# A hybrid decoder layer: more places for two weight streams, pinned scale steps two units apart, transpositions a unit later

## The chip, the cores and the metric

The kernel runs on one core of one Trainium2 chip. The metric is device time in microseconds (us). A core has five engines with a queue each, worked in order: TensorE (PE, with its weight loads as PEld), VectorE (DVE), ScalarE (ACT), GpSimd (POOL) and SyncE (SP), whose queue here issues most DMAs. Matmuls write to PSUM, a memory of eight banks per partition; the other operands lie in SBUF.

## What is computed

One layer, 2048 positions of width 1024, in float32 from outside. Cut to what matters:

```
mod = silu(c) @ w_ada + b_ada          -> sh1, sc1, g1, sh2, sc2, g2
h   = rmsnorm(x) * (1 + sc1) + sh1
q, k, v, forget, x_in, B, C = split(h @ w_in)
q, k = rmsnorm per head (8 heads of 64)
attn = causal attention with logits q.k/8 + F[t] - F[s],  F = cumsum(log sigmoid(forget + b))
conv = B * causal_dwconv3(C * x_in)
x   = x + g1 * (concat(attn, conv) @ w_out)
h2  = rmsnorm(x) * (1 + sc2) + sh2
u   = causal_dwconv3(h2 @ w_up);  x + g2 * ((silu(u_gate) * u_val) @ w_down)
```

## The kernel before, in words

A float32 product is made of three products of parts: each operand is split into a high and a low half, and high x high, high x low and low x high are added in one PSUM bank (`mm3`, L140). In the input projection most parts are float16. So that they fit float16's range, each group of weight columns is first scaled by a power of two that is worked out on the chip, and so is h.

**The planner.** The kernel is written with a framework that orders the instructions of each engine itself, by a model of their times: an instruction that is ready early can be put ahead of others that stand before it in the program. `K` (L138) pins an instruction behind the one traced before it on its engine. All of TensorE's instructions around the change are pinned, most of VectorE's and ScalarE's are not. A pool gives each tag a number of places (`bufs`); a tile waits until the last reader of its place is done.

**Value stage** (some 20 to 163 us). A loop over k = 0 to 9 makes, for each 128 rows of w_ada's first two parts, the modulation of that slice (`modulation`, L288; its columns a1 and sh1), transposes chunk 0 of x (512 positions) to h (`transpose_in`, L345), and adds the products for the values of the first three tiles of 128 positions (`value_products`). In the last rounds `normalize` (L329) squares the tiles of the next chunk on ScalarE and works out their reciprocal roots on VectorE in small steps (`rsqrt_steps`). `rest()` is the low half of h's chunk 0 (L356). Chunk 0 is multiplied in split float32, the other chunks in float16. For these `first_scales` (L368) works out two scales, of h and of the value columns: sums and maxima on VectorE (L372 to L376), a transposition (L170), a maximum (L172, L173), a small product that spreads it (L176), five small steps to the power of two (L177 to L181), then a1 and sh1 times the scale (L382, L383) and eight splits of value weights (L195 on ScalarE, L196 on VectorE). It is a generator: each `next` does a part of it. Before, its first part stood after the loop and the rest in tile 3 at k = 2. Then come 16 tiles of 128 positions; the chunks 1 to 3 are normalized and transposed between their products (L348 on TensorE, L350 on ScalarE, L136 on POOL and L353 on VectorE for the halves).

**Keys and queries** (163 to 361 us). `project` (L601) runs over 16 units, tiles of 128 positions: 24 matmuls (L142), then the squares on ScalarE (L632), sums and reciprocal roots on VectorE (L634 to L637) and the normalized tile qn (L638). `finish` (L603) transposes a qn on TensorE (L606), scales it (L612 on ScalarE), makes halves (POOL, and L614 on VectorE) and stores them by SP's queue (L616). It is called at the end of a unit's products for the tile of two units before. The dictionary of hooks puts small steps at the end of given units: the sums of the forget gates (`running_sum`, `running_offset` with the product L525), the scales of gains and values (`largest_value` with the transposition L562, and others). In the query stage each unit also loads a tile of values, splits and stores it (L578, L583, L584).

**Groups of weights.** `weight_group` (L198) is a generator that loads a group, sums magnitudes, then goes through the chain L170 to L181 in two parts, one `next` apart, and then makes the splits, one per `next`. The group of the queries is prepared during the keys, that of a conv group during the stage before it.

**Conv groups** (361 to 626 us). Four groups of 128 channels, four chunks each, and per chunk the products x, c and b (24 matmuls each); after each product one `next` of the following group. Then the gating and the convolution on POOL and VectorE (L796 to L816), and a store by ScalarE's queue.

**Two streams beside these stages.** `magnitudes` (L704) loads w_up in 88 tiles `wx` of 128 x 512 and adds up their absolute values on ScalarE (L708), for a scale of later use; it is called twice in most units and after most products of a conv group. `piece` (L691) goes through 16 pieces of the rest of w_ada: `modulate` (L654) loads eight tiles `wm` of 128 x 256, adds them up on VectorE (L662, L664), and returns a step that finishes the sum on TensorE (L669 or L684) at the next call. Calls stand in the query stage after units 3, 6, 9, 12 and 15 and in each conv chunk but the first. `wx` has one place and `wm` two.

**PSUM.** The tag "tr" has two places (`ps_t`); every transposition and every small product named here takes one until VectorE or ScalarE has read it. Accumulators have six.

At (j, ch) = (3, 2) the pool of the attention's queries and keys is opened on the right side of SBUF, and head 0's are loaded (L757) and copied by POOL (L766). The stages after 626 us (attention, output projection, ConvFFN) are not touched.

Of the kernel before, what the change touches and what calls it, by code (L numbers as in the profile page):

```python
# [45 lines left out]
def kernel(  # L46
# [102 lines left out]
    with ExitStack() as ph:  # L149
# [16 lines left out]
        def power_of_two(pool, m, s, top):  # L166
# [5 lines left out]
            V.tensor_reduce(top[:, 0:1], pt[0:n, 0:P], axis=AX.X, op=ALU.max)  # L172
            V.tensor_scalar(top, ident[0:n, 0:n], top[:, 0:1], None, op0=ALU.mult)  # L173
# [3 lines left out]
            V.tensor_scalar(s, pt[:, 0:n], 2.0**-18, 2.0**40, op0=ALU.max, op1=ALU.min)  # L177
            V.tensor_scalar(s.bitcast(I32), s.bitcast(I32), 0x7F800000, None, op0=ALU.bitwise_and)
            V.reciprocal(s, s)
            V.tensor_scalar(s.bitcast(I32), s.bitcast(I32), 0x7F800000, None, op0=ALU.bitwise_and)  # L180
            V.tensor_scalar(s, s, 4096.0, None, op0=ALU.mult)  # L181
# [16 lines left out]
        def weight_group(srcs, shape, tag):  # L198
# [7 lines left out]
            def steps():  # L206
# [11 lines left out]
                yield  # L218
                next(chain, None)
# [3 lines left out]
                for raw in raws:  # L223
# [4 lines left out]
                    yield  # L228
# [8 lines left out]
        def conv_group(j):  # L237
# [5 lines left out]
                [P, 4, P], ("wh", "wl")[j % 2],  # L243
            )

        with ExitStack() as pa:
# [121 lines left out]
            def first_scales():  # L368

                t, u = [ap.tile([P, KD], F32, tag=n, name="abs") for n in ("abs_a", "abs_s")]  # L370
                for src, dst in ((a1, t), (sh1, u)):
                    V.tensor_scalar(dst, src, -1.0, None, op0=ALU.mult)  # L372
                    V.tensor_tensor(dst, dst, src, op=ALU.max)
                V.scalar_tensor_tensor(t, t, 32.0, u, op0=ALU.mult, op1=ALU.add)
                V.tensor_reduce(hm[:, 0:1], t, axis=AX.X, op=ALU.max)
                V.tensor_reduce(hm[:, 1:2], wsum, axis=AX.X, op=ALU.max)  # L376
# [4 lines left out]
                V.tensor_copy(rh, hs[:, 0:1])  # L381
                V.tensor_scalar(a1, a1, rh, None, op0=ALU.mult)  # L382
                V.tensor_scalar(sh1, sh1, rh, None, op0=ALU.mult)  # L383
                for k in range(KD):
# [3 lines left out]
                    wv16.append(pair)  # L388
                unscale(hs[:, 1:2], hm[:, 0:1], hm[:, 1:2])
# [6 lines left out]
            early = [[ps_m.tile([P, 512], F32, tag="mm", name="pv") for _ in range(2)] for _ in range(3)]  # L396
            for k in range(KD + 2):
                if k < KD:
                    modulation(k, () if k else normalize(0))
                if 0 < k <= KD:  # L400
                    rest()
                if k < KD:
                    rest = transpose_in(0, k)
                if k == KD - 1:
                    load_x(1)
                    load_x(2)
                    norms = normalize(1)
                    next(norms)
# [1104 lines left out]
```

## Time and profile before

| | |
|---|---|
| median of 3 runs | 2441.19 us (2439.45 to 2441.63) |
| profiled execution, its own time | 2440.35 us |
| its span, first to last instruction | 2438.5 us |
| mean granted TensorE clock | 0.995 |
| loads of wx: count, KB each, issue to landing | 88, 256.0, 2.8 us |
| loads of wm: count, KB each, issue to landing | 128, 128.0, 2.7 us |
| one sum of wx on ScalarE (L708) | 629 ns |

The profile shows one execution. A row of waits reads: engine, line and tile of the instruction that waited, what ended the wait, total us, number of waits, longest. A row of a timeline reads: start and length in us, engine, line, operation, output and inputs, sizes, count, and in brackets the idle time before it and what ended it. Busy times of TensorE come from modelled ends of pipelined matmuls. A granted clock below 1.00 means that TensorE ran slower in that stretch.

### The profile page before, as it was taken

Reading aid. Unit: us, or ns where it says so; the run is one execution under the profiler, and the core shown is the slowest. Engines: PE = TensorE matmul, PEld = TensorE weight load, DVE = VectorE, ACT = ScalarE, POOL = GpSimd, SP = SyncE. Lnnn points to the kernel's source line nnn. Section 1 sums busy time; section 2 is a strip of 40 time slices with the busy share of each in tenths; the row PEclk is TensorE's granted clock in tenths of the full one; section 3 lists DMA queues with packets and bytes.
Section 4 is the critical chain, followed back from the end, with each engine's and each line's share of the span. In section 5 each row is a group of like instructions: output and inputs, shape, how many; then the busy total and the mean of one; then the engine's idle time right before and its main releaser. Section 6 shows DMA issues by size and latency. Waiting matters only on the chain.

```text
span 2438.5 us, 38643 instructions
## 1 busy us (share of the span) xinstructions
PE 2336.2 (96%) x14472; PEld 1405.9 (58%) x14472; DVE 1802.1 (74%) x3430; ACT 1307.1 (54%) x2136; POOL 338.6 (14%) x282
## 2 busy tenths in 40 slices
PE   5899989999899998999999999999999999999999
PEld 5764444444577776444444444788864444448887
DVE  6767785553799898456888888757768888985554
ACT  5644454321588897343665665554546556554333
POOL 0210101111577784001000000000000000000000
PEclk9999999999999999999999999999999999999999
DMA  9337687541599997534222222676742222236775
GB/s 278 126 105 193 156 244 208 157 127 44 109 182 187 227 183 144 179 108 151 82 92 87 87 87 86 201 247 217 229 134 87 87 87 88 92 103 210 229 227 183
DMA packets 428707, 368.71 MB, mean 151 GB/s; under 512 B 184208, under 2 KB 327912, under 8 KB 427496
## 3 DMA queue, kind: packets, MB, share of 16 engines
q1 hardware_dynamic: 421400, 349.40, 51.4%
q10 hardware_dynamic: 4752, 8.46, 1.0%
q0 software_dynamic: 2368, 8.39, 0.9%
q8 instruction: 113, 1.85, 0.3%
q14 instruction: 74, 0.61, 0.1%
HBM read 267.54 MB, written 65.08 MB: 136 GB/s over the span
## 4 chain that ended last, share of the span: by engine, by line
PE 72%; DVE 4%; ACT 2%; issue 2%; DMA 1%; POOL 0%; SPq 0%; ACTq 0%; DVEq 0%
PE acc L1360 33%; PE acc L142 24%; PE pr L142 6%; PE pt L1041 2%; PE ps L980 1%; PE ps L981 1%; DVE near L1048 1%; PE po L1077 1%; PE po L1079 1%; PE po L1078 1%; ACT s_t L1021 1%; DMA far<-wide 1%; DVE s_t L1004 1%; PE pt L1201 1%; DVE t L1177 0%
## 5 line engine op out<-in xcount | busy, mean ns | idle before, releaser
L1360 PEld LDWEIGHTS <-pair 128*128 128x128 f16 x3696 | 361.4, 98 | 436.3 <-issue 0.3
L1360 PE MATMUL acc<-t,pair 128*128 128x512 f16 x2112 | 477.4, 379 | 0.0
L1360 PE MATMUL acc<-b,pair 128*128 128x512 f16 x1584 | 363.5, 379 | 0.0
L1332 DVE TENSOR_TENSOR lo<-raw,hi 128x1024 fp32r<-128x1024 f32 x176 | 212.0, 1224 | 154.2 <-ACT hi L1331 153.9
L142 PE MATMUL acc<-hi 128*128 128x512 f32 x704 | 277.0, 394 | 1.6 <-DVE t L1177 1.5
L1331 ACT ACTIVATE hi<-raw 128x1024 fp32r<-128x1024 f32 x176 | 182.3, 1055 | 177.5 <-PE acc L142 142.4
L142 PE MATMUL acc<-lo,hi 128*128 128x512 f32 x704 | 274.5, 390 | 0.5 <-DVE lo L1332 0.5
L142 PE MATMUL acc<-hi,lo 128*128 128x512 f32 x704 | 274.4, 390 | 0.0
L1373 DVE SCALAR_TENSOR_TENSOR w<-w,fcw,w 128x1024 f32<-128x1024 f32 x176 | 226.1, 1285 | 34.6 <-ACT w L1368 25.2
L142 PEld LDWEIGHTS <-h 128*128 128x128 f16 x1344 | 130.6, 98 | 98.8 <-DVE h L353 4.6
L1184 ACT ACTIVATE pair<-raw 128x1024 f16<-128x1024 f32 x132 | 138.3, 1049 | 68.4 <-DVE raw L1267 68.4
L1368 ACT ACTIVATE w<-w,fcw 128x1024 f32<-128x1024 f32 x88 | 100.7, 1144 | 130.7 <-DVE w L1266 130.7
L142 PE MATMUL acc<-wp,mp 128*128 128x512 f16 x768 | 169.4, 379 | 1.1 <-DVE raw L933 1.0
L1021 ACT ACTIVATE s_t<-s_t,nb,cst 128x2048 f32<-128x2048 f32 (+15 forms) x128 | 164.7, 1288 | 5.1 <-ACT nb L1018 0.4
L1187 DVE TENSOR_TENSOR pair<-raw,pair 128x1024 f16<-128x1024 f32 x132 | 160.9, 1219 | 4.7 <-ACT pair L1184 4.7
L708 ACT ACTIVATE wx<-wx 128x512 f32<-128x512 f32 x88 | 55.4, 629 | 178.8 <-DMA wx<-in_w_up_dram 156.1
L142 PEld LDWEIGHTS acc<-hi 128*128 128x128 f32 x704 | 132.2, 188 | 31.4 <-DVE t L1177 4.4
L142 PEld LDWEIGHTS acc<-hi,lo 128*128 128x128 f32 x704 | 132.2, 188 | 27.8
L142 PEld LDWEIGHTS acc<-lo,hi 128*128 128x128 f32 x704 | 132.3, 188 | 27.5 <-DVE lo L1332 1.1
L1033 POOL TENSOR_TENSOR wide<-s_t,wide 128x1024 f16<-128x1024 f32 x64 | 136.7, 2136 | 5.3
L1004 DVE CUSTOM_DVE_ANT_0 s_t<-ps,nf,mx 128x512 f32<-128x512 f32 (+1 forms) x192 | 119.5, 644 | 16.6 <-PE ps L983 8.2
L142 PE MATMUL pr<-h,wl 128*128 128x512 f16 x576 | 127.0, 382 | 0.0
(344 smaller groups left out, 4212.3 us busy)
## 6 DMA issues: line engine op xcount, KB each, us to landing
raw<-in_w_up_dram SPq DMA_DIRECT2D x88, 512.0 KB, 3.7
raw<-y_sc SPq DMA_DIRECT2D x176, 256.0 KB, 4.1
raw<-in_w_down_dram SPq DMA_DIRECT2D x176, 256.0 KB, 5.9
wx<-in_w_up_dram SPq DMA_DIRECT2D x88, 256.0 KB, 2.8
y_sc<-w SPq DMA_DIRECT2D x44, 512.0 KB, 2.6
wm<-in_w_ada_dram SPq DMA_DIRECT2D x128, 128.0 KB, 2.7
wr<-in_w_in_dram SPq DMA_DIRECT2D x40, 256.0 KB, 4.2
x_t<-in_x_dram SPq DMA_DIRECT2D x16, 512.0 KB, 4.6
```

The lines of the kernel that those rows point to most:

```text
L142: ins = T.matmul(acc, lhsT=a, rhs=b, start=st, stop=sp)
L708: K(A.activation(t, t, AF.Abs, accum_out=l1[:, n : n + 1]))
L1004: K(V.tensor_tensor_reduce(out=s_t[:, o0 + c0 : o0 + c0 + cw], in0=ps[:, 0:cw], in1=nf[:, c0 : c0 + cw], scale=1.0, scalar=-3.0e38 if g == ...
L1021: K(A.activation(cols, cols, AF.Exp, bias=nb[:, p : p + 1], scale=qk[:, 4:5], accum_out=un["l"][:, p : p + 1]))
L1033: K(G.tensor_tensor(wide[:, 1, :], s_t[:, WB * P : WU], wide[:, 0, :], op=ALU.subtract))
L1184: K(A.activation(hi, raw, AF.Copy))
L1187: K(V.tensor_tensor(lo, raw, hi, op=ALU.subtract))
L1331: K(A.activation(hi, raw, AF.Copy))
L1332: K(V.tensor_tensor(lo, raw, hi.bitcast(F32), op=ALU.subtract))
L1360: K(T.matmul(acc, lhsT=a, rhs=b, start=st, stop=sp, skip_group_check=True))
L1368: K(A.activation(y, u[:, 0:1024], AF.Copy, scale=fcw[:, ct : ct + 1]))
L1373: K(V.scalar_tensor_tensor(y, u[:, m : m + 1024], fcw[:, m * 44 + ct : m * 44 + ct + 1], y, op0=ALU.mult, op1=ALU.add))
```

## The change

Five things are changed together.

- `wm` gets 16 places and `wx` four, in a pool of their own on the right side, which is closed where the attention's pool is opened. A piece's eight tiles are loaded at one call, summed at the next, and finished at the one after that; a tile of w_up is summed when three are loaded.
- In `weight_group` one more `next` lies between the two parts of the scale chain, and the conv groups from the second on make two splits per `next`.
- The VectorE instructions of the scale chains are pinned with `K`.
- `first_scales` starts in the value loop (parts at k = 7, 8 and 8), and its last four splits follow in tile 3 at k = 0; `normalize(1)` starts at k = 8, behind the last `rest()`.
- `finish` is called when three tiles of qn wait rather than two; qn has four places; three tiles are left over at the end of each projection. `running_offset` moves from unit 5 to unit 4.

The diff, without the lines that only gain a `K(...)` (L172, L173, L177 to L181, L372 to L376, L381 to L383):

```diff
-        def weight_group(srcs, shape, tag):
+        def weight_group(srcs, shape, tag, at_once=1):
...
                 next(chain)
                 yield
+                yield
                 next(chain, None)
...
-                for raw in raws:
+                for n, raw in enumerate(raws, 1):
...
-                    yield
+                    if n % at_once == 0:
+                        yield
...
-                [P, 4, P], ("wh", "wl")[j % 2],
+                [P, 4, P], ("wh", "wl")[j % 2], 2 if j else 1,
...
+                yield
                 chain = power_of_two(ps_t, hm, hs, htop)
                 next(chain)
                 yield
                 next(chain, None)
...
+                yield
                 for k in range(KD):
...
                     wv16.append(pair)
+                    if k == 3:
+                        yield
...
+            first = first_scales()
             for k in range(KD + 2):
                 if k < KD:
                     modulation(k, () if k else normalize(0))
                 if 0 < k <= KD:
+                    if k == KD:
+                        next(first)
                     rest()
...
                     load_x(2)
+                    next(first)
+                if k == KD:
                     norms = normalize(1)
                     next(norms)
                 if k >= 2:
                     for t in range(3):
                         value_products(early[t], 0, t, k - 2)
+                        if k == KD and t == 1:
+                            next(first)
...
-            first = first_scales()
             next(first)
             pin(norms)
...
-                            if (i, k) == (3, 2):
+                            if (i, k) == (3, 0):
                                 next(first)
...
+        loads = tc.tile_pool(name="lp", bufs=1, side="right")
+        lp = loads.__enter__()
...
-                    if k == MID and len(normed) == 2:
+                    if k == MID and len(normed) == 3:
                         finish(*normed.pop(0))
...
-                qn = bp.tile([P, H, DH], F32, tag="qn", name="qn")
+                qn = bp.tile([P, H, DH], F32, tag="qn", name="qn", bufs=4)
...
+        def load_ada(m):
+
+            col, q = (3, 4, 2, 5)[m // 4] * D, m % 4
+            wms = [lp.tile([P, 256], F32, tag="wm", name="wm", bufs=16) for _ in range(KD)]
+            for k, wm in enumerate(wms):
+                nc.sync.dma_start(wm, w_ada[k * P : (k + 1) * P, col + q * 256 : col + (q + 1) * 256])
+            return col, q, wms
...
-            for k in range(KD):
-                wm = bp.tile([P, 256], F32, tag="wm", name="wm")
-                nc.sync.dma_start(wm, w_ada[k * P : (k + 1) * P, col + q * 256 : col + (q + 1) * 256])
+            for k, wm in enumerate(wms):
...
+            if ahead:
+                pieces.append(modulate(*ahead.pop(0)))
             if taken[1] < 16:
-                pieces.append(modulate(taken[1]))
+                ahead.append(load_ada(taken[1]))
...
-            while up_tiles:
+            while len(up_tiles) == 3 or seen[0] == 88 and up_tiles:
...
-                t = bp.tile([P, 512], F32, tag="wx", name="wx", bufs=1)
+                t = lp.tile([P, 512], F32, tag="wx", name="wx", bufs=4)
...
-        last_k = project(..., {..., 3: running_sum, 5: running_offset, ...}, (0, 13), group)
+        last_k = project(..., {..., 3: running_sum, 4: running_offset, ...}, (0, 13), group)
...
-        last_q = project(..., {0: last_k, 1: last_k, 3: piece, ...}, (2, 15), convs[0][2])
+        last_q = project(..., {0: last_k, 1: last_k, 2: last_k, 3: piece, ...}, (2, 15), convs[0][2])
...
                 if j == 3 and ch == 2:
+                    loads.__exit__(None, None, None)
                     sp = st.enter_context(tc.tile_pool(name="sp", bufs=2, side="right"))
...
-                        if (j, ch, k) == (0, 0, MID) and name in "xc":
+                        if (j, ch, k) == (0, 0, MID):
                             last_q()
...
-                bt = bp.tile([P, 512], F32, tag="qn", name="bt")
+                bt = bp.tile([P, 512], F32, tag="qn", name="bt", bufs=4)
```

More of the change, by code (lines that the diff above doesn't have):

```diff
@@ L171, in power_of_two @@
             top = top[0:n, 0:n]
-            V.tensor_reduce(top[:, 0:1], pt[0:n, 0:P], axis=AX.X, op=ALU.max)
-            V.tensor_scalar(top, ident[0:n, 0:n], top[:, 0:1], None, op0=ALU.mult)
+            K(V.tensor_reduce(top[:, 0:1], pt[0:n, 0:P], axis=AX.X, op=ALU.max))
+            K(V.tensor_scalar(top, ident[0:n, 0:n], top[:, 0:1], None, op0=ALU.mult))
             yield
@@ L687, in modulate @@
             return columns if col in (3 * D, 4 * D) else rows
-        pieces = []
+        pieces, ahead = [], []
         def piece():
@@ L704, in magnitudes @@
         def magnitudes():
[L706 removed]
+            while len(up_tiles) == 3 or seen[0] == 88 and up_tiles:
                 n, t = up_tiles.pop(0)
                 K(A.activation(t, t, AF.Abs, accum_out=l1[:, n : n + 1]))
[L709 to L711 removed]
+            if seen[0] < 88:
+                n = seen[0]
+                t = lp.tile([P, 512], F32, tag="wx", name="wx", bufs=4)
                 k, i = divmod(n, 11)
@@ L747 @@
         w_q, u_q, group = columns_of(0, "wl")
-        last_k = project(w_k, u_k, AW, gq[:, 1:2], k_hi, k_lo, {0: largest_gains, 1: gain_scales, 3: running_sum, 5: running_offset, 7: largest_value, 9: value_scale}, (0, 13), group)
+        last_k = project(w_k, u_k, AW, gq[:, 1:2], k_hi, k_lo, {0: largest_gains, 1: gain_scales, 3: running_sum, 4: running_offset, 7: largest_value, 9: value_scale}, (0, 13), group)
         convs = [conv_group(0)]
-        last_q = project(w_q, u_q, 0, gq[:, 0:1], q_hi, q_lo, {0: last_k, 1: last_k, 3: piece, 6: piece, 9: piece, 12: piece, 15: piece}, (2, 15), convs[0][2])
+        last_q = project(w_q, u_q, 0, gq[:, 0:1], q_hi, q_lo, {0: last_k, 1: last_k, 2: last_k, 3: piece, 6: piece, 9: piece, 12: piece, 15: piece}, (2, 15), convs[0][2])
         def load_head(h):
```

32 lines of the change are left out of this document (15 added, 17 removed).

## The prediction

> **What bounds the kernel now.** I read the page's busy times first, then busy time by stage, then TensorE's waits in the stages that the diff touches, then the waits of the engines that feed it.
>
> ```profile
> span 2438.5 us, 38643 instructions
> PE 2336.2 (96%) x14472; PEld 1405.9 (58%) x14472; DVE 1802.1 (74%) x3430; ACT 1307.1 (54%) x2136; POOL 338.6 (14%) x282
> ```
>
> TensorE bounds the whole: it idles 2438.5 - 2336.2 = 102.3 us in all, and no change of order can bring more than that. The diff works between 50 and 626 us. By stage (keys, queries, first two conv groups, last two; columns: length, busy PE, PEld, DVE, ACT, POOL, granted clock, DMA share, GB/s):
>
> ```profile
> 163.00:263.00 100.00, 96.75 (x478) 47.38 (x476) 78.02 (x315) 42.17 (x99) 9.64 (x17) 1.00 0.61 167
> 263.00:361.00 98.00, 89.63 (x444) 44.44 (x444) 81.35 (x294) 48.70 (x103) 10.05 (x17) 0.98 0.79 214
> 361.00:427.00 66.00, 65.48 (x315) 30.82 (x315) 37.88 (x101) 28.02 (x66) 7.67 (x10) 1.00 0.76 212
> 427.00:499.00 72.00, 66.61 (x303) 30.93 (x301) 38.21 (x86) 23.34 (x55) 8.31 (x9) 0.95 0.51 152
> 499.00:626.00 127.00, 127.00 (x591) 58.29 (x589) 53.65 (x98) 23.10 (x48) 18.62 (x17) 1.00 0.24 73
> ```
>
> TensorE idles 3.25, 8.37, 0.52, 5.39 and 0 us: 17.5 us. The waits of TensorE, first in the stretch from 55 to 95 us (value stage), then from 163 to 626 us (columns: total, times, longest):
>
> ```profile
> PE pt L348 <- ACT hf L350: 6.4, 2, 6.2
> PE pv L142 <- DVE hl L356: 2.4, 1, 2.4
> PE pv L142 <- DVE h L353: 1.7, 2, 1.2
> ...
> PE pt L606 <- DVE qn L638: 5.8, 6, 1.9
> PE pt L176 <- DVE group L173: 5.4, 1, 5.4
> PE pt L606 <- DVE rqt L127: 2.5, 1, 2.5
> PE po L525 <- DVE group L172: 2.3, 1, 2.3
> PE pt L606 <- ACT sq L632: 1.6, 1, 1.6
> ```
>
> All 17.6 us of the second list belong to things that the diff names: transpositions of normalized keys and queries (L606: 5.8 + 2.5 + 1.6 = 9.9), the scale step (L176), and the step that had to find a free place of "tr" behind it (L525). Why those were late shows in the waits of ScalarE and VectorE from 163 to 626 us:
>
> ```profile
> ACT wx L708 <- DMA wx<-in_w_up_dram: 156.1, 69, 5.3
> ACT vo L583 <- DMA vt<-v_sc: 19.0, 11, 3.6
> ...
> DVE mo L664 <- DMA wm<-in_w_ada_dram: 59.5, 51, 3.1
> ```
>
> Both engines run their queues in order. The one place of wx and the two of wm make each load wait for the use of the one before, so the squares, normalizations and split halves queue behind a DMA.
>
> **Part A, the value stage** (scale chain begun before the end of chunk 0's products, four of its eight splits later, `normalize(1)` after the last `rest()`). From the timelines of VectorE and ScalarE (start us, length us, engine, line, operation, count, idle before):
>
> ```profile
> 60.20 0.17 DVE L336 TENSOR_SCALAR ss<-ss 128x4 f32<-128x4 f32 x1 [5.22 <-ACT junk L335]
> 64.68 0.15 DVE L123 TENSOR_SCALAR rb<-ss 128x4 int32<-128x4 int32 x1
> 67.43 2.74 DVE L343 TENSOR_SCALAR x_t<-x_t,ss 128x1024 f32<-128x1024 f32 x4
> 72.89 5.06 ACT L195 ACTIVATE wv<-wvr,scales 128x520 f16<-128x520 f32 x8 [1.31 <-DVE scales L181]
> 73.65 5.46 DVE L196 SCALAR_TENSOR_TENSOR wv<-wvr,scales,wv 128x520 f16<-128x520 f32 x8
> ```
>
> Now L356 sits behind L336, which waits for four squares of x: the 2.4 us wait. Moving `normalize(1)` behind it removes this. The scale's pinned L177 then follows L336 on VectorE; L177 and its four following steps take 0.2 us each (as rsqrt's twelve and one more do between 64.68 and 67.43), so the scale is there near 61.5, not 72.9. Four splits take 4 x 0.63 on ScalarE, the last low half is done near 64.7, and the pinned rsqrt follows it: 67.43 - 64.68 = 2.75, less what other work took in between, so 2.1 to 2.75, then 2.74 for x_t. So x_t is ready near 69.5 to 70.2, as now (70.2). TensorE, which comes there 2.4 us sooner, waits for x_t: that saving is spent at once. But L350 of chunk 1, which stands behind eight splits until 72.89 + 5.06 = 77.95, now starts after x_t, its first transposition and one eviction of values, near 71.5. That is 6.4 us less; the other four splits (2.7 us on VectorE) may get between it and the first low half. I take 6. Bounds: 1, if all eight splits are placed ahead of the normalization and of L350; 10, if all three waits of the list (10.5) go. The clock after such a wait is no term here: the new wait for x_t costs it likewise.
>
> **Part B, transpositions a unit later** (L606, and four places of qn). A unit is (98 - 8.4) / 16 = 5.6 us, and the longest wait is 2.5 us, so each single wait is covered. Their sum, 9.9, is more than one unit; if VectorE fell behind for good, only 5.6 would go. It doesn't: it is busy 81.35 of 98 us, the 59.5 us spent on wm go, and since a piece is now loaded at one call, summed at the next and finished at the third, one piece fewer falls into the query stage. I take 9 of 9.9; bounds 5 and 9.9.
>
> **Part C, running_offset a unit earlier, scale steps two apart.** The 2.3 us at L525 go: only L606 uses "tr" beside it in unit 4. But L176 of the query group now comes in unit 7, ahead of `largest_value`, so L606, L176 and L562 want three of two places, as L606, L170 and L525 do now. L562 waits until ScalarE has read L606's tile (two pairs from the timelines):
>
> ```profile
> 184.62 0.60 PE L606 MATMUL pt<-ident,qn 128*128 128x128 f32 x4
> ...
> 204.53 0.60 PE L606 MATMUL pt<-ident,qn 128*128 128x128 f32 x4
> ...
> 185.31 0.68 ACT L612 ACTIVATE tf<-pt,gq 128x512 f32<-128x512 f32 x1
> ...
> 207.16 0.68 ACT L612 ACTIVATE tf<-pt,gq 128x512 f32<-128x512 f32 x1
> ```
>
> The tile is free 1.4 us (185.99 - 184.62) to 3.3 us after L606 begins, and TensorE is ready for L562 after L606's 0.60 and a short L176, say 0.8 in all: a new wait of 0.6 to 2.5. I take 0.8, near the case in which ScalarE wasn't held by wx. C = 2.3 - 0.8 = 1.5 (bounds -0.2 and 1.7).
>
> **Parts D and E, the conv stage and the clock.** The 5.4 us at L176 end a chain of wx and wm loads, each issued only when ScalarE or VectorE gave a place back. With L176 a product later (5.2 us) and no such loads to wait for, it should vanish. Two stretches also ran slowly, by TensorE's timeline:
>
> ```profile
> 340.57 0.63 PE L606 MATMUL pt<-ident,qn 128*128 128x128 f32 x4 [1.85 <-DVE qn L638]
> 341.40 7.03 PE L142 MATMUL acc<-wl,h 128*128 128x512 f16 x24
> 348.70 5.34 PE L142 MATMUL acc<-wl,h 128*128 128x512 f16 x24
> 465.22 17.23 PE L142 MATMUL pr<-h,wl 128*128 128x512 f16 x72
> 482.72 15.70 PE L142 MATMUL pr<-h,wl 128*128 128x512 f16 x72
> ```
>
> and the busy time by stretch (columns as above) gives the clock there:
>
> ```profile
> 340.60:345.00 4.40, 4.40 (x18) 2.12 (x19) 4.12 (x18) 1.45 (x3) 0.00 (x0) 0.66 1.00 278
> 463.70:468.00 4.30, 4.28 (x11) 2.17 (x12) 2.99 (x10) 0.00 (x0) 1.30 (x2) 0.50 0.25 84
> ```
>
> After the wait of 1.85 us one unit took 7.03 instead of 5.34 at a granted clock of 0.66; after the 5.4 us, 17.23 instead of 15.70 at 0.50. Without the waits 1.7 (E) and 1.5 come back. D = 5.4 + 1.5 = 6.9 (bounds 5.4 and 6.9); E = 1.7 (bounds 0 and 1.7). [...]
>
> **Edits at nothing.** The pinned scale steps can hold VectorE's queue while they wait for TensorE's small product, and the normalizations queue behind them. From 0 to 620 us this happens now as
>
> ```profile
> DVE group L177 <- PE pt L176: 4.1, 2, 3.7
> ```
>
> so it costs VectorE at most 3.7 us for each of six groups, less than the 5.6 us by which L606, the one that waits for it, was put off. `finish` takes its copy on POOL and its two stores on SP's queue along: they land a unit later, and the last is issued one product later in the first conv chunk, long before a head reads it. The same 88 and 128 loads and sums are issued; three wx sums in a row now come at the end (3 x 0.63 us on ScalarE, mostly idle there). The new pool lies on the right side, where head 0's and head 1's queries and keys are loaded afterwards, so these loads can't run ahead in the key and query stages any more; they have to follow the last use of wx and wm (timelines of ScalarE, POOL, TensorE):
>
> ```profile
> 564.87 0.63 ACT L708 ACTIVATE wx<-wx 128x512 f32<-128x512 f32 x1 [1.23 <-DVE y L815]
> ...
> 592.35 2.46 POOL L766 TENSOR_SCALAR kh<-kh 64x2048 f16<-64x2048 f16 x1
> ...
> 627.05 0.38 PE L980 MATMUL ps<-kh,qs 128*128 128x512 f16 x1 [0.69 <-issue]
> ```
>
> From 565 to the copies at 592 there are 27 us, and the DMA engines are idle for three quarters of that stage (share 0.24), so it is hidden. Without this cover the copies and the attention's first product would slip, one us for one, from a landing later than 622 on (627 less two copies of 2.46).
>
> **Sum.** 6 + 9 + 1.5 + 6.9 + 1.7 = 25.1 us. The profiled execution took 2440.35 us (1.85 around the span), so it becomes 2415.2; the median of the runs, 2441.19, stands 0.8 above it: 2416. After 626 us nothing is touched, and TensorE is the bound, so what is won earlier arrives at the end. With every part at its low bound the gain is 1 + 5 - 0.2 + 5.4 + 0 = 11.2 (2430), at its high bound 10 + 9.9 + 1.7 + 6.9 + 1.7 = 30.2 (2411).
>
> **Rivals.**
> 1. *The value stage gives nothing*: the pins put splits ahead of the normalization, and x_t, not L350, holds TensorE. For it: rsqrt is pinned behind four splits. Against: ScalarE is then free when x_t is done. 2422; 0.11.
> 2. *VectorE is the bound of the query stage*: B and E give back about 9. For it: 81.35 of 98 us busy, in chains of small dependent steps. Against: the 8.4 us by which TensorE idles leave it idle time too. 2425 to 2427; 0.09.
> 3. *The loads ahead do nothing*, because the DMA engines and not the places set their pace: B, D and E stay out, 2416 + 17.6 = 2434. For it: a share of 0.79 in the query stage. Against: 214 GB/s there, and 278 in the row at share 1.00; 0.04.
> 4. *Slower*: eight loads of a piece now go out together on SP's queue, 1.05 MB or 3.8 us at 278 GB/s, and the value tile's load stands behind them; L583 waits for it (19.0 us now), and VectorE's split of that tile behind L583. If the five calls in the query stage cost TensorE those 3.8 us each, B and E bring nothing and 19 us come on top: 2441 - 6 - 1.5 - 6.9 + 19 = 2446. It decides from 2.9 us a call on (14.4 / 5). Against: the bytes are the same, and the three units of lead take 16.8 us. 0.03.
> 5. *No change*, gains and new waits cancelling, 2441: 0.03.
>
> **How the numbers follow.** The forecast has 0.70, with 2410 to 2421 as its own range. The range 2409 to 2427 takes in rivals 1 and 2 and leaves out some 0.15. A change under 0.2% (4.9 us) can't be told from none. Faster: forecast and rivals 1 to 3, 0.94, less a little for a rival 3 with a weak A: 0.93. Same 0.04, slower 0.03.
>
> **What would show it.** Right: no wait of ScalarE on wx or of VectorE on wm over a few us in all; L606 waits under 1 us in sum; TensorE busy over 97 of each 98 us of the query stage, its clock 1.00; one wait of about a us at L562; one of some 5 us for x_t near 65 us in place of the 6.2 us at L350; the head's loads issued after the last wx. Wrong: waits of L606 that stay (rival 2), L350 still behind eight splits (rival 1), L583 waiting longer than 19 us (rival 4), or a first L980 that waits for POOL's copies.

## The result and the profile after

The changed kernel took 2412.43 us (median of 4 runs, 2407.69 to 2414.95), the kernel before 2440.32 on the same chip (4 runs, 2439.35 to 2441.63): a ratio of 0.9883, 95% interval 0.9866 to 0.9900. The profiled execution took 2413.08 us. The page of the changed kernel begins:

```profile
span 2411.3 us, 38606 instructions
PE 2328.6 (97%) x14472; PEld 1403.3 (58%) x14472; DVE 1804.9 (75%) x3430; ACT 1304.2 (54%) x2136; POOL 338.5 (14%) x282
```

Line numbers have moved: the transposition L606 of before is L620 here, its copy L612 is L626, wx L708 is L729, L348, L350 and L353 of the value stage are L350, L352 and L355, L583 is L597. Busy time by stretch (columns as in the prediction; keys and queries end near 338, the last conv group near 596):

```profile
155.00:255.00 100.00, 99.48 (x499) 49.72 (x498) 84.14 (x342) 43.97 (x104) 10.64 (x18) 1.00 0.62 172
255.00:350.00 95.00, 95.00 (x483) 48.29 (x481) 86.96 (x310) 52.45 (x117) 10.48 (x17) 1.00 0.84 238
350.00:415.00 65.00, 65.00 (x312) 30.63 (x311) 34.46 (x74) 26.24 (x63) 8.47 (x10) 1.00 0.66 196
415.00:480.00 65.00, 65.00 (x309) 30.40 (x307) 35.16 (x80) 19.96 (x46) 7.30 (x9) 1.00 0.48 146
480.00:596.00 116.00, 115.92 (x539) 53.66 (x537) 51.81 (x95) 20.26 (x41) 17.97 (x17) 1.00 0.28 84
```

Behind the value stage TensorE idles 0.52 us up to 350 us and 0.08 from there to 596, and its clock is 1.00 throughout. The starts of the stages, by the first TensorE instruction of each in the two timelines, say where the 27.2 us of the span came from:

| | before | after | change in length |
|---|---|---|---|
| keys begin | 162.94 | 156.03 | value stage -6.9 |
| queries begin | 257.72 | 247.09 | keys -3.7 |
| first conv group | 361.01 | 338.57 | queries -11.8 |
| second conv group | 426.62 | 403.64 | first -0.5 |
| third conv group | 498.69 | 467.91 | second -7.8 |
| attention begins | 627.05 | 596.65 | third and fourth +0.4 |
| end of the span | 2438.5 | 2411.3 | all the rest +3.2 |

So 30.4 us are won up to the attention, and 3.2 are lost behind it, where nothing was edited. What TensorE still waits for, in the value stage (55 to 95 us) of the changed kernel:

```profile
PE pv L142 <- ACT vt L466: 3.4, 2, 3.1
PE pv L142 <- DVE h L355: 2.7, 4, 1.2
PE pt L350 <- ACT hf L352: 0.5, 2, 0.3
PE pv L142 <- POOL h L136: 0.5, 1, 0.5
PE pt L350 <- DVE x_t L345: 0.3, 1, 0.3
```

Of the 6.4 us for `hf` 0.5 are left, and the 2.4 for `hl` are gone; a wait of 3.1 us for `vt`, the eviction of a value tile, is new. From 156 to 612 us there is nothing for L620 or the scale step L176; of the steps named in the diff one remains, L576 (L562 of before), in TensorE's timeline:

```profile
200.21 0.60 PE L620 MATMUL pt<-ident,qn 128*128 128x128 f32 x4
...
201.63 0.27 PE L576 MATMUL pt<-ident,vm 128*1 128x128 f32 x1 [0.52 <-ACT tf L626]
```

It waits for ScalarE's reading of the tile that L620 has just filled:

```profile
200.90 0.68 ACT L626 ACTIVATE tf<-pt,gq 128x512 f32<-128x512 f32 x1
```

The view that explains the most is one that the prediction didn't use: all of ScalarE's waits in the query stage. Before (263 to 361 us):

```profile
ACT wx L708 <- DMA wx<-in_w_up_dram: 23.9, 17, 2.9
ACT vo L583 <- DMA vt<-v_sc: 18.1, 10, 3.6
...
ACT sq L632 <- PE acc L142: 1.0, 1, 1.0
```

And after (247 to 338.5 us):

```profile
ACT sq L646 <- PE acc L142: 22.1, 8, 4.4
ACT vo L597 <- DMA vt<-v_sc: 15.5, 11, 3.5
```

Before, ScalarE was busy for 48.70 of 98 us and waited 42.0 for these two loads; for TensorE's products it waited once, 1.0 us. An engine that takes a product from TensorE in every unit and finds it done in all but one of them runs behind TensorE. After, it waits 22.1 us for TensorE, in eight waits: the pace is TensorE's again. The row alone doesn't clear VectorE, which has no listed wait for TensorE in this stage, before or after; it works behind ScalarE's squares (5.3 us of waits for `sq` before, 4.4 after). The runs with one of the two loads at a time, below, tell the two engines apart.

### The profile page after: what moved, and what is told of

Read it like the earlier page. It is cut to its first block, busy times and chain, and to the rows that moved or that the text cites. A ratio compares the mean times of both kernels' runs of the same rounds, so it can differ in the third digit from the quotient of the medians.

```text
span 2411.3 us, 38606 instructions
## 1 busy us (share of the span) xinstructions
PE 2328.6 (97%) x14472; PEld 1403.3 (58%) x14472; DVE 1804.9 (75%) x3430; ACT 1304.2 (54%) x2136; POOL 338.5 (14%) x282
## 3 DMA queue, kind: packets, MB, share of 16 engines
q8 instruction: 113, 1.85, 0.3%
## 4 chain that ended last, share of the span: by engine, by line
PE 85%; DVE 7%; ACT 3%; issue 2%; DMA 2%; POOL 0%; SPq 0%; DVEq 0%; ACTq 0%; POOLq 0%
PE acc L1383 33%; PE acc L142 30%; PE pr L142 10%; PE pv L142 2%; PE pt L1064 2%; PE ps L1003 1%; PE ps L1004 1%; DVE near L1071 1%; PE po L1100 1%; DVE s_t L1027 1%; PE po L1102 1%; PE po L1101 1%; ACT s_t L1044 1%; DMA far<-wide 1%; DMA raw<-in_w_down_dram 1%
## 5 line engine op out<-in xcount | busy, mean ns | idle before, releaser
L142 PEld LDWEIGHTS <-mp 128*128 128x128 f16 x768 | 75.1, 98 | 88.7 <-issue 2.9
L142 PE MATMUL pr<-h,wh 128*128 128x512 f16 x576 | 126.5, 379 | 0.0
```

The source lines that it names most:

```text
L142: ins = T.matmul(acc, lhsT=a, rhs=b, start=st, stop=sp)
```

## The experiments

Twelve runs, in four batches (e2 to e5; e1, e6, e7, e8; e9 to e11; e12). A time is compared with the kernel before in the same batch (2441.41, 2439.83, 2443.41 and 2440.09 us); the same program's median differs by some 3 us between batches. Starts are read as in the table above; the last column is the start of the attention.

| run | us | ratio (interval) | keys | first conv | attention |
|---|---|---|---|---|---|
| e2_loads_only | 2417.80 | 0.9902 (0.9888-0.9917) | 161.88 | 345.41 | 603.71 |
| e3_later_only | 2440.66 | 0.9995 (0.9986-1.0005) | 163.24 | 361.44 | 627.64 |
| e4_no_later | 2412.80 | 0.9887 (0.9870-0.9903) | 155.47 | 339.57 | 597.43 |
| e5_no_loads | 2434.95 | 0.9969 (0.9956-0.9983) | 156.51 | 351.13 | 617.37 |
| e1_value_only | 2435.09 | 0.9976 (0.9967-0.9986) | 155.59 | 352.11 | 620.61 |
| e6_loads_and_value | 2411.89 | 0.9883 (0.9866-0.9899) | | | |
| e7_wx_only | 2424.28 | 0.9930 (0.9913-0.9947) | 163.87 | 348.47 | 612.38 |
| e8_splits_later | 2410.04 | 0.9875 (0.9860-0.9889) | 154.97 | 336.94 | 595.02 |
| e9_loads_and_value_again | 2413.84 | 0.9883 (0.9867-0.9900) | 155.96 | 339.98 | 598.48 |
| e10_changed_again | 2409.06 | 0.9862 (0.9847-0.9876) | 155.91 | 338.45 | 596.53 |
| e11_splits_later_again | 2409.48 | 0.9866 (0.9851-0.9881) | 155.61 | 337.58 | 595.66 |
| e12_wm_only | 2433.95 | 0.9970 (0.9958-0.9982) | 163.93 | 360.83 | 620.20 |

**The loads alone, the lead alone.** Does the unit of lead carry part B, as predicted, or the loads ahead? The first kernel is the one before with the loads edit alone:

```
-                t = bp.tile([P, 512], F32, tag="wx", name="wx", bufs=1)
+                t = lp.tile([P, 512], F32, tag="wx", name="wx", bufs=4)
...
+            wms = [lp.tile([P, 256], F32, tag="wm", name="wm", bufs=16) for _ in range(KD)]
...
+            if ahead:
+                pieces.append(modulate(*ahead.pop(0)))
```

> The kernel before, with the loads ahead alone (16 places of wm, four of wx, their own pool). Theory (the waits on single places made the transpositions and the scale step late): TensorE's waits at the transpositions of queries and keys fall from 9.9 us to under 3, the 5.4 us at the scale step of the second conv group go with 1.5 of clock, the 2.3 us at running_offset and the value stage stay: about 15 us less, 2425. Rival (only the additional unit of lead helps): transpositions still wait 6 us or more, only the conv stage gains, 2433. Rival (VectorE is the bound): waits as before, 2438.

The second is the one before with the lead alone:

```
-                    if k == MID and len(normed) == 2:
+                    if k == MID and len(normed) == 3:
...
-                qn = bp.tile([P, H, DH], F32, tag="qn", name="qn")
+                qn = bp.tile([P, H, DH], F32, tag="qn", name="qn", bufs=4)
```

> The kernel before, with the transpositions of queries and keys a unit later alone (finish at three, four places of qn). Theory: each single wait was at most 2.5 us and the lead is 5.6 us more, so they go whatever made them late: waits there under 1 us, with their clock 11 to 13 us less, 2428; the 5.4 us in the conv stage and the value stage stay. Rival (VectorE is the bound): the sum of 9.9 is only put off, at most 5.6 us go, 2434 or more. Rival (the loads alone matter): nothing moves, 2439.

The loads alone brought 23.6 us, more than the 15 expected, and the lead alone 0.8, with an interval that holds zero. TensorE's waits in the kernel with the lead alone, 150 to 625 us:

```profile
PE pt L176 <- DVE group L173: 8.1, 3, 5.0
PE pm L669 <- ACT tf L612: 6.5, 2, 3.5
PE po L525 <- DVE group L172: 1.8, 1, 1.8
PE pt L606 <- DVE sh L674: 0.9, 1, 0.9
```

L606 is down from 9.9 us to 0.9, as predicted. But the four lines make 17.3 us, and before it was 17.6: L606 lost 9.0 us, and L669, L176 and L525 together gained 8.7. The waits only changed their names. One of them in that kernel's timelines, first TensorE:

```profile
336.44 0.60 PE L606 MATMUL pt<-ident,qn 128*128 128x128 f32 x4
339.97 0.60 PE L669 MATMUL pm<-ones,mo 128*128 128x1 f32 x4 [2.93 <-ACT tf L612]
```

then ScalarE:

```profile
335.03 0.63 ACT L708 ACTIVATE wx<-wx 128x512 f32<-128x512 f32 x1 [1.02 <-DMA wx<-in_w_up_dram]
...
337.10 0.63 ACT L191 ACTIVATE junk_w<-wr 128x512 bf16<-128x512 f32 x1 [1.35 <-DMA wr<-in_w_in_dram]
...
338.62 0.63 ACT L708 ACTIVATE wx<-wx 128x512 f32<-128x512 f32 x1 [0.80 <-DMA wx<-in_w_up_dram]
...
339.25 0.67 ACT L612 ACTIVATE tf<-pt,gq 128x512 f32<-128x512 f32 x1
```

The transposition comes on time at 336.44, but ScalarE reads its tile only at 339.25, behind work that waited for the loads of `wr`, a weight tile, and of wx; until then the place of "tr" is taken, and the next small product, L669, waits for it. Ahead of the other wait of L669 (3.53 us, at 360.98) it is a wx alone, 1.85 us. Of the 8.1 us at L176, 5.0 are the wait of the second conv group, which was there before. In the query stage of this kernel ScalarE waited 28.0 us for wx and has no wait for TensorE at all. With the loads ahead alone, TensorE's waits on the same steps, 150 to 625 us, are these (L527 is the L525 of before, L608 its L606):

```profile
PE po L527 <- ACT tf L614: 0.7, 1, 0.7
...
PE pt L608 <- DVE qn L640: 0.2, 1, 0.2
```

**The changed kernel without the one and without the other.** Without the lead (`len(normed) == 2`, two places of qn, two leftovers):

> The changed kernel without the transpositions a unit later (finish at two again). If the loads ahead had already removed what made them late, the transpositions wait under 3 us in sum and the time is 2413 to 2416. If the lead carries the gain of the key and query stages, they wait 6 to 10 us and the time is 2419 to 2424.

and without the loads ahead (wx in one place, wm in two, each piece loaded and summed at one call):

> The changed kernel without the loads ahead (one place of wx, two of wm, pieces loaded and summed at one call, as before). If the lead alone carries the key and query stages, the transpositions still wait under 1 us; the scale step of the second conv group, now a product (5.2 us) later, waits 0 to 2 us: 2413 to 2417. If the loads carry it, waits of 5 us or more come back in the query stage and 3 or more in the conv stage: 2420 to 2425.

Without the lead nothing measurable is lost; the attention begins 0.8 us later. Without the loads ahead only 6.5 us of the gain are left, less than either side of the expectation gave, and TensorE's waits (150 to 625 us) are these:

```profile
PE pt L176 <- DVE group L173: 5.9, 1, 5.9
PE pm L681 <- ACT tf L624: 4.5, 2, 3.7
PE pt L574 <- ACT tf L624: 4.2, 1, 4.2
```

Two of the three are again a place of "tr" that ScalarE hasn't read.

**The value stage alone**, and with the loads. The edit is the reordering of `first_scales` and of the calls around it, as in the diff, together with the pins of the scale chains, which all later groups share; the pins weren't run alone.

> Only the change in the value stage (scale chain begun before the end of chunk 0's products, four of the eight splits later, normalize(1) after the last rest()); everything behind it as before. Theory (the parts add): the keys start near 156 us instead of 162.9, the waits of the query and conv stages stay as they were, and the time is 2440.3 - 6.9 = 2433.5, bounds 2432 to 2436. Rival (what is won here is spent at the next wait, since the queues of ScalarE and VectorE stand behind loads that keep their own pace): the keys start early, but the queries start at 257 as before, and the time is 2438 to 2441.

> The value stage and the loads ahead, without the unit of lead for the transpositions, without the extra step between the scale's two halves, with running_offset where it was. Theory (these two edits are the whole): 2417.8 - 6.9 = 2410.9, that is the changed kernel's time within its spread, bounds 2409 to 2415; L606's and L176's waits stay under 1 us each. Rival (the extra step and the lead carry part of it once the keys start earlier): 2416 to 2420, with one or two waits of 2 to 5 us back at the scale step.

> The value stage and the loads ahead once more, for a profile that can be read. Theory (these two edits are the whole of the change, the lead and the extra step carry nothing): the keys start at 155 to 156.5 us, the queries near 247 to 248.5, the first conv group near 339 to 341; L606, the scale step and the steps behind it wait under 1.5 us in all; time 2410 to 2414. Rival (the lead or the extra step still carries a wait that falls elsewhere): one wait of 2 us or more at the scale step, and the first conv group not before 342.

Alone it moved the keys from 162.94 to 155.59 us and the attention by 6.4 us, and 4.7 us arrived at the end, within the bounds expected; the stages between keep their waits, 16.3 us in all. With the loads ahead it reaches the ratio that the whole change had at first, 0.9883 both times. (The profiled execution of e6 came out at 10,087.55 us, with no listed wait of TensorE from 40 to 95 and from 130 to 615 us; why isn't known, no line of it is read here, and e9 is the same kernel again.) These two edits are most of the whole: in the batch of e9 and e10 they won 29.6 of 34.4 us. The lead, the extra step, two splits at a time and the earlier running_offset are worth 1.95 us in the start of the attention (598.48 against 596.53). The medians of that batch differ by more, 4.8 us, and why isn't settled.

**One load at a time.** Only wx in four places, each tile summed three calls of `magnitudes` after its load instead of one, and only wm ahead; the fences show the line with the places:

```
-                t = bp.tile([P, 512], F32, tag="wx", name="wx", bufs=1)
+                t = lp.tile([P, 512], F32, tag="wx", name="wx", bufs=4)
```

> The kernel before with four places for the tiles of w_up alone (ScalarE's loads); w_ada keeps its two places and its load and sum at one call. Theory (ScalarE, with 156 us of waiting for these loads, was what held the tr places and the squares): most of the 22.5 us of loads alone, 2419 to 2424, and VectorE still waits for wm for 40 to 60 us. Rival (VectorE's sums of w_ada, which stand ahead of the normalizations and scale steps, carried as much): half, 2427 to 2432, with waits of TensorE for normalizations (qn) and for the scale step (group) that stay.

```
-                wm = bp.tile([P, 256], F32, tag="wm", name="wm")
+            wms = [lp.tile([P, 256], F32, tag="wm", name="wm", bufs=16) for _ in range(KD)]
```

> The kernel before with the tiles of w_ada alone loaded ahead (sixteen places, load, sum and finish at three calls); w_up keeps its one place. The places of w_up alone brought 2439.83 - 2424.28 = 15.6 us, both together 22.5. Theory (ScalarE behind its loads is the main cause, VectorE's sums a smaller one, and each removes its own waits): 22.5 - 15.6 = 7 us, 2431 to 2436, the wait at the scale step of the first conv group shorter or gone, L606's waits for ScalarE (sq, tf) left. Rival (the two loads hold each other up, and freeing either one frees most): 2420 to 2428. Rival (VectorE's loads are nothing by themselves as long as ScalarE waits): 2438 to 2441.

wx alone brought 15.6 us, wm alone 6.1; the sum, 21.7, is near the 23.6 of both: each load carries its own part. (The 22.5 in e12's expectation sets both loads against the kernel before of another batch.) Whether fewer places would do as well wasn't tried. With wx ahead ScalarE waits 22.2 us for TensorE in the query stage, as in the changed kernel, L606 and L525 (here L608 and L527) wait 0.7 us each, and what is left is mostly VectorE's (TensorE's waits, 150 to 625 us):

```profile
PE pt L176 <- DVE group L173: 3.5, 1, 3.5
```

VectorE still waits 2.0 us for wm in that query stage, against 1.7 before, and yet the stage takes 92.70 us instead of 103.29; with wm alone it takes 103.09. So it was ScalarE, behind wx, that made the query stage late. The wait at L176 now comes one conv group earlier, at 384.19 us: the first group takes 71.08 us instead of 65.61, the second 64.43.

With wm alone it is the other way round. L176 waits no more, the second conv group takes 64.35 us instead of 72.07 and the first 66.19, but L527 (L525 of before) and L608 (L606) still stand behind ScalarE or the normalization:

```profile
PE po L527 <- ACT tf L614: 5.2, 1, 5.2
PE pt L608 <- DVE rqb L123: 2.7, 1, 2.7
PE pt L608 <- DVE qn L640: 2.3, 3, 1.3
```

**The new wait of the value stage.** In the changed kernel tile 3's products wait for one of six accumulators. ScalarE's timeline shows why:

```profile
61.15 2.58 ACT L195 ACTIVATE wv<-wvr,scales 128x520 f16<-128x520 f32 x4 [1.11 <-DVE scales L181]
63.64 0.36 ACT L466 ACTIVATE vt<-pv 128x260 f32<-128x260 f32 x1
```

The eviction L466 stands behind four splits. In the next kernel the first four splits come after the second tile's eviction, and `largest_value` a unit later:

```
-            next(first)
             pin(norms)
...
+                    if i == 1:
+                        next(first)
...
-{..., 7: largest_value, ...}
+{..., 8: largest_value, ...}
```

> The changed kernel, with the first four splits of the value weights put behind the second tile's eviction instead of ahead of the first, the normalization of chunk 1 pinned ahead of them, and largest_value a unit later. Theory (tile 3's products wait 3.1 us for an accumulator, whose eviction stands behind four splits on ScalarE): that wait goes, of 3.4 us some 2.5 are won, and 0.5 more at the largest_value step: 2409 to 2410. Rival (chunk 1's products then wait for the splits that come later, or for low halves behind them on VectorE): the wait comes back at the first product of chunk 1, and the time is 2412 to 2414.

> The changed kernel with the first four splits behind the second eviction and largest_value a unit later, once more, beside the changed kernel on the same chip. Theory (the keys start 1.06 us sooner and the conv groups 1.6 us sooner than in the changed kernel): 1 to 2 us below the changed kernel's median of this call. Rival (what is won is lost again in stretches of half clock): within 0.5 us of it.

Its waits in the value stage, 55 to 95 us:

```profile
PE pv L142 <- DVE h L355: 4.5, 4, 2.0
PE pt L350 <- DVE x_t L345: 1.2, 4, 0.3
```

The wait for `vt` is gone, but 2.7 us of it came back, at the low halves of h on VectorE and at x_t. The keys begin 0.3 us (e11 against e10) to 1.1 us (e8 against the changed kernel) sooner, the attention 0.9 to 1.6. Beside the changed kernel on one chip the time is the same, 2409.48 (2408.27 to 2413.21) against 2409.06 (2408.12 to 2409.96). By its waits the rival of e8's expectation is the nearer one, and by its time e11's rival (within 0.5 us): it isn't a better kernel by any margin that was measured.

**The 3.2 us lost behind the attention's start.**

> The changed kernel once more, to see what stays the same between two profiles of one program. Theory (the 3.2 us that it lost behind 597 us are chance: where stretches of half clock fall, and how long loads from far take): the lead of 30.4 us at the first product of the attention stays within 0.5, while the length from there to the end lies anywhere from 1811.5 to 1815, with stretches of half clock at other places. Rival (the loss belongs to the change): the length is 1814.5 or more again, with the stretch of half clock at the same wait, near 1068 us.

The second profile of the same program begins the attention at 596.53 us, 0.12 from the first, and needs 1811.07 us from there instead of 1814.65; the theory's range began at 1811.5. One difference can be pointed at, a transposition in the output projection. In the first profile:

```profile
1067.90 1.12 PE L1224 MATMUL pt<-ident,w 128*128 128x128 f32 x4 [2.16 <-ACT t L1226]
```

and in the second:

```profile
1066.03 0.66 PE L1224 MATMUL pt<-ident,w 128*128 128x128 f32 x4 [2.17 <-ACT t L1226]
```

The same wait; after the one the four transpositions take 1.12 us, after the other 0.66, and from there to the next transposition 15.09 and 13.44 us pass. The clock around it (1050.80 to 1070.80 us) in the first and in the second:

```profile
1050.80:1070.80 20.00, 17.84 (x85) 8.99 (x83) 12.35 (x20) 9.33 (x15) 0.00 (x0) 0.93 0.11 31
```

```profile
1050.80:1070.80 20.00, 17.83 (x91) 8.99 (x90) 13.06 (x21) 10.03 (x16) 0.00 (x0) 1.00 0.13 40
```

That is 1.7 of the 3.6 us, what 3.41 us at a granted clock of 0.50 (1067.88 to 1071.29 us, in the last section) cost. Another difference is a wait for loads of the attention, over 612 to 1900 us, in the first and in the second:

```profile
PE po L1100 <- DMA far<-wide: 3.3, 4, 1.6
```

```profile
PE po L1100 <- DMA far<-wide: 1.6, 3, 0.7
```

That is 1.7 us more, if it reaches the end whole. So the loss doesn't belong to the change: one program showed both lengths, the kernel before needs 1811.5, and in the thirteen profiles that can be read the length lies anywhere from 1810.9 to 1814.7.

## Why the prediction was right in the sum, and wrong in a step

The time predicted, 2416, is 0.15% above the 2412.43 measured. By its own steps:

- **A, the value stage, 6 us: the size held, by another route.** 6.9 in the profile, 7.35 where the edit was made alone (without it the profiled kernels begin the keys between 161.88 and 163.93 us). The chain came as worked out, the scale's L181 at 60.95 us (predicted 61.5), x_t done at 70.6 (69.5 to 70.2), ScalarE's L352 at 71.03 (71.5); by the changed kernel's timelines of VectorE

```profile
60.95 0.17 DVE L181 TENSOR_SCALAR scales<-scales 128x2 f32<-128x2 f32 x1
...
67.88 2.73 DVE L345 TENSOR_SCALAR x_t<-x_t,ss 128x1024 f32<-128x1024 f32 x4
```

  and ScalarE

```profile
71.03 0.78 ACT L352 ACTIVATE hf<-pt,sh,a 128x512 f32<-128x512 f32 x1 [1.92 <-PE pt L350]
```

  Two things were otherwise. "TensorE, which comes there 2.4 us sooner, waits for x_t" named the wrong releaser: x_t costs 0.3 us, and the wait of 3.1 is for an accumulator behind the splits. And the clock was said to be no term here, since the new wait would cost it likewise. Busy time and clock from 55 to 95 us, before and after:

```profile
55.00:95.00 40.00, 28.21 (x199) 24.55 (x198) 27.70 (x62) 27.93 (x52) 7.07 (x8) 0.87 0.64 212
```

```profile
55.00:95.00 40.00, 32.54 (x254) 27.90 (x254) 32.89 (x83) 33.48 (x68) 7.00 (x8) 0.96 0.64 224
```

  The clock rose from 0.87 to 0.96; 0.09 of 40 us is up to 3.6 us at full clock. The listed waits fell by 4.3 us (11.7 to 7.4, the small ones of before included). These two, not the "6.4 us less" at L350 alone, make up A, and a little more than it, since part of the slow time lay in waits (from 75.40 to 82.30 us of the kernel before, at a clock of 0.53, TensorE was busy for 3.64 of 6.90 us).
- **B, transpositions a unit later, 9 us: this is the step that failed.** The prediction said that "a unit is 5.6 us, and the longest wait is 2.5 us, so each single wait is covered". The waits of L606 were indeed covered, and it brought nothing that was measured: with the lead alone 9.0 us went from L606 and 8.7 came up at other instructions, and without the lead the changed kernel's attention begins only 0.8 us later. The 9 us would have needed an engine that is late now and then, not one that falls behind for good. The prediction asked whether one did of VectorE alone, and answered with the 59.5 us that it spends on wm, of which 1.7 lie in the query stage. The engine that did was ScalarE: behind its loads of wx it found TensorE's product done in all but one unit of the query stage. What removed the waits was the loads ahead, wx above all. That the sum came out all the same is luck in this part: the edit that B was credited to and the edit that earned it stand in the same change. Rival 3 came near it by the number: it let B fall with the loads and gave 2434, and the kernel without the loads took 2434.95. Its reason, that the DMA engines set the pace, is not borne out: the loads alone won 23.6 us.
- **C, 1.5 us: came to 1.8, a little over its high bound of 1.7.** The wait at L525 went, and the new wait at L562 is 0.52 us against 0.8 taken and 0.6 to 2.5 as bounds; ScalarE reads L620's tile at once now, done 1.37 us after L620 begins. But L525 fell to 0.7 us with the loads alone, running_offset unmoved, so the move carries little.
- **D, the wait and the clock of the second conv group, 6.9 us: the wait went as predicted**, and 7.8 were measured, above the high bound of 6.9. It is wm's, and needs no extra step between the scale's halves: wm alone shortens the first two conv groups together from 137.68 to 130.54 us, wx alone to 135.51. The term was too small since it counted the half clock (0.50 from 463.70 to 468.00 us) for the products alone. L176 and L684 (L703 in the changed kernel) in front of them ran slowly too, in the kernel before:

```profile
463.72 0.55 PE L176 MATMUL pt<-group,ones 1*128 1x1 f32 x2 [5.39 <-DVE group L173]
464.21 1.22 PE L684 MATMUL pm<-mo,ones 128*128 128x256 f32 x2
```

  Each counted to the next start, they took 0.49 and 1.01 us (the products begin at 465.22), and in the changed kernel 0.31 and 0.44: 0.75 us more.
- **E, 1.7 us for the half clock after a wait of 1.85 us: held;** the granted clock of that stage is 1.00 now, against 0.66 from 340.60 to 345.00 us before. Its low bound of 0 had no row beside it. Rows of before do show waits that cost no clock: 2.33 us at L525 (ended at 199.11 us) and 2.47 at L606 (315.69) lie in a stretch at 1.00 (in the last section). And of the pair of profiles above, 2.16 us cost half clock the one time and 2.17 nothing the other.
- **B to E together** were 19.1 us and came to 23.5. What was missing in the sum is, most of all, how a wait ends. In the lead-alone kernel 24 matmuls are listed with 5.34 us, and the next instruction begins 5.18 us after they do:

```profile
331.26 5.34 PE L142 MATMUL acc<-wl,h 128*128 128x512 f16 x24
336.44 0.60 PE L606 MATMUL pt<-ident,qn 128*128 128x128 f32 x4
```

  So the last 0.16 us of the listed time overlap with the next work there. Ahead of a wait they don't: in the kernel before 24 matmuls listed from 333.38 us with 5.34 end at 338.72, and the wait of 1.85 us is counted from there to 340.57. Ten waits make the 17.6 us of before, and with 0.16 for each 1.6 us come on top, an estimate from these two cases. Another 1.2 come because the waits went whole, but for the 0.52 (17.1, and 3.2 for the clock, against the 19.1 taken), and 0.75 are those of D. The last 0.9 us were not traced.
- **The signs:** TensorE is busy in the query stage and the clock is 1.00, as said. But ScalarE still waits 16.2 us for wx from 156 to 597 us, not a few: 15.6 of them lie in the conv groups, where TensorE waited for nothing listed.
- **At nothing:** the head's loads behind the last wx cost nothing; the first L1003 waits 0.7 us, and for VectorE. Rival 4's row, `vo` for the value tile's load, went from 19.0 to 21.7 us over the same stages, but TensorE didn't wait for it.
- **Behind 626 us**, "what is won earlier arrives at the end" held within the 3.6 us by which two profiles of one program differ there.

## What to carry to other kernels

Before a step on the bound engine is given more lead, look at the engine that feeds it. If that one spends its time on work and on waits for loads and hardly ever waits for the bound engine, suspect that it sets the pace; then, as here, lead only moves the wait to the next instructions that need it (9.0 us went from L606, 8.7 came up at others). Sum the waits over the whole stage, not those of the line that was moved. And put a streaming load that stands in the same queue as the feeding work into several places first; here that was most of the gain outside the value stage (23.6 us alone, 15.6 of them with wx alone).

## What the runs showed of the hardware that was not expected

Waits of about one length cost half clock in one case and nothing in another. In the first profile of the changed kernel, around the transposition that waited 2.16 us (columns as in the prediction):

```profile
1064.47:1067.88 3.41, 1.26 (x8) 0.69 (x6) 2.10 (x5) 1.94 (x4) 0.00 (x0) 1.00 0.26 77
1067.88:1071.29 3.41, 3.39 (x10) 1.75 (x11) 2.76 (x6) 2.78 (x5) 0.00 (x0) 0.50 0.49 142
1071.29:1074.70 3.41, 3.41 (x17) 1.56 (x16) 3.15 (x5) 0.43 (x1) 1.06 (x2) 1.00 0.30 92
```

TensorE is busy for 1.26 of the 3.41 us up to the end of the wait; then the clock is 0.50 for 3.41 us, and 1.00 again. In the second profile TensorE is busy, by its timeline, for 1.24 of the 3.41 us up to the end of the same wait (2.17 us, ended at 1066.03), and the clock is 1.00 from 1050.80 to 1070.80 us. In the kernel before half clock follows the wait of 1.85 us (ended at 340.57), while the waits of 2.33 and 2.47 us lie in a stretch at 1.00:

```profile
163.00:342.00 179.00, 167.89 (x836) 82.97 (x835) 143.42 (x551) 82.60 (x185) 17.74 (x30) 1.00 0.69 186
338.60:342.01 3.41, 1.56 (x12) 1.15 (x12) 3.10 (x10) 1.02 (x3) 0.62 (x1) 1.00 1.02 298
342.01:345.42 3.41, 3.41 (x9) 1.18 (x8) 3.13 (x15) 0.91 (x3) 0.00 (x0) 0.50 0.96 253
345.42:348.83 3.41, 3.41 (x19) 1.84 (x18) 2.85 (x9) 2.21 (x5) 0.62 (x1) 1.00 0.86 253
```

So the length of the wait didn't decide it in these cases; what did isn't shown.

The half clock came in two lengths. By the clock records in the traces of the two kernels, and but for the last microseconds of each, the changed kernel has it in two more stretches,

```profile
64.36:67.77 3.41, 3.04 (x15) 2.73 (x14) 3.14 (x15) 3.41 (x7) 0.00 (x0) 0.50 0.99 297
924.52:927.93 3.41, 3.41 (x44) 3.35 (x41) 1.42 (x3) 2.69 (x5) 0.00 (x0) 0.50 0.20 45
```

and the kernel before in four more:

```profile
62.11:65.52 3.41, 3.41 (x19) 3.33 (x18) 1.15 (x8) 0.73 (x3) 0.00 (x0) 0.50 0.89 123
75.77:82.60 6.83, 3.94 (x19) 3.62 (x20) 6.32 (x9) 6.53 (x11) 2.26 (x3) 0.50 0.92 296
461.47:468.30 6.83, 4.58 (x12) 2.27 (x13) 4.83 (x16) 1.30 (x3) 1.69 (x2) 0.50 0.28 79
952.99:956.40 3.41, 2.88 (x41) 2.82 (x41) 2.16 (x6) 1.95 (x3) 0.00 (x0) 0.50 0.43 79
```

All eight are 3.41 or 6.83 us long. In the changed kernel their starts lie 860.16 and 1003.52 us behind the first, 252 and 294 times 3.413 us.
